# The boundary between gate-up groups: the order of pair 6's banks, of the additions and of pair 7's products

## The chip, the cores and the metric

The kernel runs on one core of a Trainium2 chip. The metric is the device time of one execution in microseconds (us). In the profile PE is TensorE's matmul, PEld its weight load, DVE is VectorE, ACT is ScalarE, POOL is GpSimd and SP is SyncE, whose queue issues most of the loads. A source line of the kernel before is named by L and its number; DMA is a transfer.

## The reference

One layer of a hybrid encoder over 256 tokens of width 2048, in float32: a feed-forward layer, a mixer (a gated linear recurrence beside windowed attention), and a second feed-forward layer of the same form.

```python
def swiglu(x, w_gate_up, w_down):
    gate, up = jnp.split(x @ w_gate_up, 2, axis=-1)
    return (jax.nn.silu(gate) * up) @ w_down
...
    ff = swiglu(rms_norm(x, pre_norm_ffn1[layer]), w_ffn1_gate_up[layer], w_ffn1_down[layer])
    x = x + 0.5 * rms_norm(ff, post_norm_ffn1[layer])
    ...
    ff = swiglu(rms_norm(x, pre_norm_ffn2[layer]), w_ffn2_gate_up[layer], w_ffn2_down[layer])
    x = x + 0.5 * rms_norm(ff, post_norm_ffn2[layer])
```

`w_gate_up` is 2048 x 11264, `w_down` 5632 x 2048. The change touches `x @ w_gate_up` alone, in both feed-forward layers.

## The kernel before

**Split products.** Each float32 operand is split into an upper part h (a cast to a shorter format, on ACT, L176) and a lower part l = raw - h (a subtraction, on DVE or POOL, L177). A full product is three matmuls: upper by upper, upper by lower, lower by upper (`three`, `some_of`, L447).

**Groups and pairs.** The gate-up matrix is worked in 11 groups of 512 gate and 512 up columns. A group sums over K = 2048 in 8 pairs of 256 rows. Its result is four banks of PSUM, 128 x 512 each: c[m][n], m the half of the tokens, n = 0 for gate and 1 for up. The names "pa" and "pb" in the profile are the two tags under which the banks are allocated; c[0][n] and p1, p5 are pa, c[1][n] and p6, p7 are pb.

**Plain pairs and pairs of seven.** A plain pair adds eight block products (24 matmuls) to the c banks. A pair of seven forms Strassen-like sums of blocks first and needs seven block products (21 matmuls): three go to c banks, four to side banks p1, p5, p6, p7, which are added to the c banks at the end of the group. Pairs 2 to 6 are of that kind in groups 3 to 10; in group 2 pairs 2, 4, 5 and 6; in group 1 some pairs, but not pair 6. Such a pair costs DVE two additions on the raw tile (L1001, L1002) and three or four subtractions; its weights come by two loads of SP and one adding load of POOL (`add_second`, L148), which `prepare` issues behind a split of the pair's first block (h1, l1).

**Order.** The engines' order is written by hand: every engine executes its instructions in the order in which the code records them (`manual_schedule`). The pools of h and l hold 5 tiles of 128 x 1024 each.

**The boundary.** `boundary` ends a group. `take` has issued pair 6's products, with `before_fold` in an order of their own. The eight additions of the side banks (through two rooms, a and b, named z and s in the profile) run on DVE, after a copy of p1 by ACT (L1259); between them stand pair 7's products, whose weights POOL has split (`splits(g, last, nc.gpsimd)`): `bank(m, n)` is the four matmuls of one bank that need no lower part of the weights (`upper`), and `lower()` the eight that do. Behind it `some(ahead, 2)` splits the next group's pair 0, and `first_pairs` goes on with the silu of the finished banks (`units`: L1176 on ACT, L1181 on DVE), the next group's pairs 0 and 1 and the transposes.

Of the kernel before, what the change touches and what calls it, by code (L numbers as in the profile page):

```python
# [17 lines left out]
ALU = mybir.AluOpType  # L18
# [30 lines left out]
def hymba_layer_kernel(  # L49
# [19 lines left out]
    nc = tc.nc  # L69
# [145 lines left out]
    last = {}  # L215
# [186 lines left out]
    class Blocks:  # L402
# [4 lines left out]
        ahead = None  # L407
# [27 lines left out]
        def bank(self, at):  # L435
            return self.p[at[1]] if at[0] == "p" else self.c[at[1]][at[2]]
# [486 lines left out]
    class Gated(Blocks):  # L923
# [91 lines left out]
        def take_parted(self, g, u):  # L1015

            (h0, l0), (h1, l1) = self.split_of.pop((g, u))
            del self.raws[g, u]
            a = self.tiles[u]

            def parts(m, n, k):
                ms = slice(m * P, (m + 1) * P)
                o = (n ^ k) * 512
                cs = slice(o, o + 512)
                return ("c", m, n), a[:, k, 0, ms], a[:, k, 1, ms], (h0, h1)[k][:, cs], (l0, l1)[k][:, cs]

            def upper(m, n):
                for k in range(2):
                    at, ah, al, h, _ = parts(m, n, k)
                    self.some_of(at, (ah, h), (al, h))  # L1030

            def lower():
                for k in range(2):
                    for n in range(2):
                        for m in range(2):
                            at, ah, _, _, l = parts(m, n, k)
                            self.some_of(at, (ah, l))

            return upper, lower

        def take(self, g, u):

            got = self.split_of.pop((g, u))
            del self.raws[g, u]
            first = self.firsts.pop((g, u), None)
            if first:
                before_fold = u == KT // 2 - 2
                self.products(u, first, *got, (0, 1, 3, 4, 5, 6, 2) if before_fold else range(7))
                return ()
            hs, ls = zip(*got)  # L1050
            return [
                (lambda k=k, m=m, n=n: self.plain(u, hs, ls, m, n, k))
                for k in range(2)
                for m in range(2)
                for n in range(2)
            ]
# [27 lines left out]
    def ffn(gated, w_dn, post_gain, again, gain=None, lead=None, opening=None):  # L1084

        with ExitStack() as st:
# [136 lines left out]
            def some(steps, n):  # L1223
                for _ in range(n):
                    next(steps)

            last = KT // 2 - 1
# [24 lines left out]
            def boundary(g, ahead):  # L1252

                a, b = room_for("z"), room_for("s")
                c, (p1, p5, p6, p7) = gated.c, gated.p
                add = nc.vector.tensor_tensor
                bank, lower = gated.take_parted(g, last)

                nc.scalar.copy(a, p1)  # L1259
                add(c[0][0], c[0][0], a, ALU.add)  # L1260
                add(b, p6, a, ALU.add)  # L1261
                add(a, p7, b, ALU.add)  # L1262
                add(c[1][0], c[1][0], a, ALU.add)  # L1263
                bank(0, 0)
                bank(1, 0)
                add(b, p5, b, ALU.subtract)
                add(c[0][1], c[0][1], b, ALU.add)  # L1267
                bank(0, 1)
                add(b, p5, a, ALU.subtract)  # L1269
                add(c[1][1], c[1][1], b, ALU.add)  # L1270
                bank(1, 1)
                lower()
                some(ahead, 2)

            def first_pairs(g, waiting, ahead):

                gated.group(g)
                sevens = FIVE if g in FIVE_IN else MIXED_IN
                if ahead:
                    some(waiting, 2)  # L1280
                    gated.prepare(g, sevens[1], nc.gpsimd)
                    some(ahead, 1)
                else:
                    some(waiting, 1)
                    gated.prepare(g, sevens[1])
                    some(waiting, 1)
                    ahead = gated.splits(g, 1)
                    some(ahead, 2)
                    gated.prepare(g, sevens[2])
                for one in gated.take(g, 0):  # L1290
                    one()
                some(waiting, 1)
                ahead = gated.splits(g, 2)
                some(ahead, 2)
                next(ahead, None)
                some(waiting, 1)
                for one in gated.take(g, 1):
                    one()
# [39 lines left out]
            raws, firsts, got = {}, {}, {}  # L1338
# [73 lines left out]
            with tc.manual_schedule():  # L1412
                if not opening:
                    gated.prepare(1, MIXED_IN[0])
                    some(gated.splits(1, 0), 2)
                begun = None
                for g in range(1, NG):
                    first_pairs(g, waiting, begun)
                    for u in range(2, last - 1):
                        pair_ahead(g, u)  # L1420
                    some(gated.splits(g, last, nc.gpsimd), 2)
                    for one in gated.take(g, last - 1):
                        one()
                    boundary(g, gated.splits(g + 1, 0) if g < NG - 1 else splits(0))
                    if g < NG - 1:
                        begun = gated.splits(g + 1, 1)
                        next(begun)
                    among = None
                    if g < NG - 1:
                        third = (FIVE if g + 1 in FIVE_IN else MIXED_IN)[2]  # L1430
                        among = lambda g=g, u=third: gated.prepare(g + 1, u, nc.gpsimd)
                    waiting = units(gated.c, rest, among)
                    some(waiting, 2)
                room_cm.__exit__(None, None, None)
                close_far()
                back_cm = tc.tile_pool(name=nm("hb"), bufs=AWAY // 2, reuse_waits="tile")
                back = back_cm.__enter__()
                fetch_at = {2: (1,), 4: (3,), 6: (0,), 8: (5,), 10: (2,), 12: (7,), 13: (4,), 15: (6,)}
                fetch_at.update({25: (3,), 26: (0,), 28: (5,), 29: (1,)})
                again_at = {4: 16, 7: 17, 10: 18, 30: 19}  # L1440
                for u in (*MIXED[8:], 17):
                    sums[u] = None
                rows = Pairs(w_dn, orders, hts, sums, work, post_gain, near=MIXED[:2])
                rows.firsts = 3
                some(waiting, 2)
                ahead = splits(1)
                some(ahead, 2)
                products(0)
                for _ in range(2):
                    load_down(back.tile([P, 2048], F32, tag="raw", name=nm("raw"), bufs=2))  # L1450
                some(waiting, 1)
                ahead = splits(2)
                some(ahead, 2)
                some(waiting, 1)
                some(ahead, 1)
                products(1)
                for i in range(2, 2 * NU - Pairs.HELD):
                    if i == NU + 18:
                        back_cm.__exit__(None, None, None)
                        early_cm.__exit__(None, None, None)  # L1460
                        post = rows.post = st.enter_context(post_pool())
                    ahead = splits(i + 1)
                    next(ahead, None)
                    prepare(i + 4)
                    for u in fetch_at.get(i, ()):
                        fetch(u)
                    next(ahead, None)
                    if i == NU + 18:
                        rows.hold(1, raws[2 * NU - 2])
                    products(i)  # L1470
                    for _ in ahead:
                        pass
                    if i in again_at:
                        sums[again_at[i]] = sums_again(again_at[i])
                    if i == 8:
                        rows.half_gain(far["pool"])
                    if i == NU - 1:
                        sums[19] = None
                        rows.second_run()
                        rows.fold_after(NU - Pairs.HELD - 1)  # L1480
                fold = rows.fold()
                some(fold, 2)
                rows.hold(1, raws[2 * NU - 1])
                for _ in fold:
                    pass
# [8 lines left out]
    gated = Gated(w_ffn1_gate_up, two_banks())  # L1494
    xt = new_xt()
    gated.see(xt)
    with tc.manual_schedule():
# [17 lines left out]
        first = gated.source(0)  # L1515
# [1043 lines left out]
```

## Time and profile before

| | us |
|---|---|
| median of 3 runs (1822.75 to 1824.27) | 1823.04 |
| the profiled execution | 1823.13 |
| its span in the profile | 1821.4 |
| PE busy | 1798.4 (99%) |
| DVE busy | 1648.0 (90%) |
| ACT busy | 1143.9 (63%) |
| POOL busy | 288.5 (16%) |

How to read it: the span is the time from the first to the last instruction of the profiled execution, and 1.7 us lie around it. The granted clock is 0.999 of full speed. PE is busy nearly all of the span, so a microsecond counts where PE idles or where its matmuls start further apart than they must. A group of the gate-up stage takes about 42.4 us (pair 6 of one group starts at 381.23, pair 6 of the next at 423.63), and there are 10 boundaries in each of the two layers. The fused rows of the timeline start at the first of their instructions and last to the end of the last.

### The profile page before, as it was taken

What the parts mean: (1) busy time and instruction counts of PE and PEld (TensorE: products, weight loads), DVE (VectorE), ACT (ScalarE), POOL (GpSimd) and SP (SyncE); (2) the same over time, 40 slices, a digit from 0 to 9 for tenths busy, and PEclk for the clock granted to TensorE, in tenths of its full rate; (3) what the DMA queues carried; (4) which work ended last, traced back from release to release, by engine and by line L of the source; (5) the groups of instructions that cost most, each with busy time, mean ns of one, the idle gap of its engine ahead of it and who ended that gap; (6) DMA issues with size and microseconds to landing.
All of it is one profiled execution on the core that took longest, in us unless ns stands there. A gap on an engine that the chain in (4) does not pass through costs nothing.

```text
span 1821.4 us, 24095 instructions
## 1 busy us (share of the span) xinstructions
PE 1798.4 (99%) x8320; PEld 1480.1 (81%) x8320; DVE 1648.0 (90%) x2154; ACT 1143.9 (63%) x1527; POOL 288.5 (16%) x270
## 2 busy tenths in 40 slices
PE   9999999999999999999999999999999999999998
PEld 7877787777788888888899888877777778788886
DVE  6899999999999999888888888889999999999997
ACT  7556666666665667566667566556666656566663
POOL 0122322222110100000000000022223222200110
PEclk9999999999999999999999999999999999999999
DMA  9789999899799997954555767889999899799895
GB/s 369 231 246 283 284 296 261 262 256 253 237 325 306 310 281 244 295 160 165 181 166 173 254 206 262 249 236 270 285 278 279 255 270 260 199 319 340 270 318 167
DMA packets 130331, 469.05 MB, mean 258 GB/s; under 512 B 14608, under 2 KB 17424, under 8 KB 128672
## 3 DMA queue, kind: packets, MB, share of 16 engines
q1 hardware_dynamic: 109152, 391.18, 59.5%
q0 software_dynamic: 20912, 76.07, 23.5%
q8 instruction: 65, 1.06, 0.2%
q14 instruction: 58, 0.48, 0.1%
q10 hardware_dynamic: 144, 0.26, 0.0%
HBM read 452.77 MB, written 14.68 MB: 257 GB/s over the span
## 4 chain that ended last, share of the span: by engine, by line
PE 86%; DVE 9%; DMA 2%; ACT 1%; issue 1%; SPq 0%; POOL 0%; DVEq 0%; ACTq 0%; POOLq 0%
PE pa L447 39%; PE pb L447 34%; PE pa L315 6%; PE pa L320 3%; DVE l L177 1%; DMA raw<-in_w_ffn_gate_up_dram 1%; ACT h L176 1%; DVE pa L1267 1%; DVE pb L1270 1%; DVE s L1269 1%; DVE z L1262 1%; DVE pb L1263 1%; PE pa L369 1%; DVE s L1261 1%; PE pa L368 1%
## 5 line engine op out<-in xcount | busy, mean ns | idle before, releaser
L176 ACT CAST h<-raw 128x1024 fp32r<-128x1024 f32 (+1 forms) x881 | 850.6, 1002 | 428.2 <-DVE raw L1002 99.8
L177 DVE TENSOR_TENSOR l<-raw,h 128x1024 fp32r<-128x1024 f32 (+1 forms) x789 | 915.6, 1191 | 64.3 <-ACT h L176 45.5
L447 PE MATMUL pa<-h,xt 128*128 128x512 f32 x1214 | 407.9, 393 | 4.3 <-DVE pa L1267 3.9
L447 PE MATMUL pb<-h,xt 128*128 128x512 f32 x1012 | 350.9, 395 | 7.2 <-DVE pb L1270 5.4
L447 PEld LDWEIGHTS pa<-h,xt 128*128 128x128 f32 x1214 | 226.3, 188 | 59.0 <-DVE pa L1267 12.8
L447 PEld LDWEIGHTS pb<-h,xt 128*128 128x128 f32 x1012 | 186.8, 188 | 61.1 <-DVE pb L1270 14.1
L447 PE MATMUL pa<-l,xt 128*128 128x512 f32 x583 | 227.6, 390 | 0.4 <-DVE l L177 0.4
L447 PE MATMUL pb<-l,xt 128*128 128x512 f32 x506 | 197.1, 389 | 0.0
L177 POOL TENSOR_TENSOR l<-raw,h 128x1024 fp32r<-128x1024 f32 (+1 forms) x76 | 142.7, 1897 | 207.7 <-ACT h L176 202.4
L447 PE MATMUL pb<-h,ht 128*128 128x512 f32 x428 | 151.2, 389 | 0.0
L447 PE MATMUL pa<-h,ht 128*128 128x512 f32 x428 | 151.1, 389 | 0.0
L148 POOL DMA_DIRECT2D raw<-in_w_ffn_gate_up_dram x93 | 81.7, 890 | 420.1 <-DVE l L177 369.5
L447 PEld LDWEIGHTS pa<-l,xt 128*128 128x128 f32 x583 | 109.5, 188 | 23.4 <-DVE l L177 1.4
L447 PE MATMUL pa<-h,xs 128*128 128x512 f32 x328 | 117.5, 389 | 0.5 <-DVE sums L399 0.5
L447 PE MATMUL pb<-h,xs 128*128 128x512 f32 x328 | 114.3, 389 | 0.0
L447 PEld LDWEIGHTS pb<-l,xt 128*128 128x128 f32 x506 | 95.0, 188 | 19.8
L315 PE MATMUL pa<-xt,h 128*128 128x512 f32 x448 | 109.9, 393 | 0.0
L315 PEld LDWEIGHTS pa<-xt,h 128*128 128x128 f32 x448 | 81.5, 188 | 15.3
L447 PEld LDWEIGHTS pb<-h,ht 128*128 128x128 f32 x428 | 80.3, 188 | 16.6
L447 PEld LDWEIGHTS pa<-h,ht 128*128 128x128 f32 x428 | 80.3, 188 | 16.6
L148 POOL DMA_DIRECT2D raw<-in_w_ffn_down_dram x42 | 36.5, 868 | 348.0 <-DVE la L177 276.8
L447 PE MATMUL pa<-l,ht 128*128 128x512 f32 x214 | 83.3, 389 | 0.0
(345 smaller groups left out, 2681.5 us busy)
## 6 DMA issues: line engine op xcount, KB each, us to landing
raw<-in_w_ffn_gate_up_dram SPq DMA_DIRECT2D x350, 512.0 KB, 6.4
raw<-in_w_ffn_down_dram SPq DMA_DIRECT2D x176, 512.0 KB, 8.5
raw<-in_w_mix_in_dram SPq DMA_DIRECT2D x94, 512.0 KB, 4.8
raw<-in_w_ffn_gate_up_dram POOLq DMA_DIRECT2D x93, 512.0 KB, 8.9
raw<-in_w_ffn_down_dram POOLq DMA_DIRECT2D x42, 512.0 KB, 8.7
ht<-away SPq DMA_DIRECT2D x24, 512.0 KB, 10.5
raw<-in_w_mix_out_dram SPq DMA_DIRECT2D x24, 512.0 KB, 5.9
away<-ht SPq DMA_DIRECT2D x16, 512.0 KB, 9.2
```

The costliest lines, as they stand in the source:

```text
L148: nc.gpsimd.dma_start(raw[:, 0:1024], src[:, 512:1536], accum_op=ALU.add)
L176: nc.scalar.copy(hi, src)
L177: by.tensor_tensor(lo, src, hi.bitcast(F32), ALU.subtract)
L315: nc.tensor.matmul(slot[f], weights(hs, kk, f), xcol(xt, k), start=(k == 0), stop=(k == KT - 1))
L320: nc.tensor.matmul(slot[f][:, 0:T], weights(ls, kk, f), xcol(xt, kh * 8 + kk, 0), start=False, stop=False,)
L368: nc.tensor.matmul(dst, xh, l[:, o : o + n], start=False, stop=False)
L369: nc.tensor.matmul(dst, xl, h[:, o : o + n], start=False, stop=(k == KT - 1))
L447: nc.tensor.matmul(self.bank(at), lhs, rhs, start=(n == 1), stop=n in (ends, self.of[at]), skip_group_check=n > ends,)
L1261: add(b, p6, a, ALU.add)
L1262: add(a, p7, b, ALU.add)
L1263: add(c[1][0], c[1][0], a, ALU.add)
L1267: add(c[0][1], c[0][1], b, ALU.add)
```

## The change

Pair 6 (`take`): its side-bank products come first (p1, p5, p7, p6) and the three products for c banks behind them; before, one c product stood in second place. Boundary: ACT copies p1 before it casts pair 7's weights, not after; the eight additions stand in one row with b = p6 + a first; and each of pair 7's banks takes its product with the first half of the lower parts right behind its four upper ones (`most`). The products with the second half follow: of three banks ahead of the last bank's products, of the last bank at the end. `first_pairs`: the second split of pair 1 (`some(ahead, 1)`) is recorded ahead of `prepare`, not behind it. No instruction is added or removed.

```diff
-            def lower():
-                for k in range(2):
-                    for n in range(2):
-                        for m in range(2):
-                            at, ah, _, _, l = parts(m, n, k)
-                            self.some_of(at, (ah, l))
+            def lower(m, n, k):
+                at, ah, _, _, l = parts(m, n, k)
+                self.some_of(at, (ah, l))
...
-                self.products(u, first, *got, (0, 1, 3, 4, 5, 6, 2) if before_fold else range(7))
+                self.products(u, first, *got, (0, 3, 4, 5, 1, 6, 2) if before_fold else range(7))
...
-                bank, lower = gated.take_parted(g, last)
-
                 nc.scalar.copy(a, p1)
+                some(gated.splits(g, last, nc.gpsimd), 2)
+                upper, lower = gated.take_parted(g, last)
+
+                def most(m, n):
+                    upper(m, n)
+                    lower(m, n, 0)
+
+                add(b, p6, a, ALU.add)
                 add(c[0][0], c[0][0], a, ALU.add)
-                add(b, p6, a, ALU.add)
                 add(a, p7, b, ALU.add)
                 add(c[1][0], c[1][0], a, ALU.add)
-                bank(0, 0)
-                bank(1, 0)
+                most(0, 0)
+                most(1, 0)
                 add(b, p5, b, ALU.subtract)
                 add(c[0][1], c[0][1], b, ALU.add)
-                bank(0, 1)
+                most(0, 1)
                 add(b, p5, a, ALU.subtract)
                 add(c[1][1], c[1][1], b, ALU.add)
-                bank(1, 1)
-                lower()
+                for m, n in ((0, 0), (1, 0), (0, 1)):
+                    lower(m, n, 1)
+                most(1, 1)
+                lower(1, 1, 1)
                 some(ahead, 2)
...
                 if ahead:
                     some(waiting, 2)
+                    some(ahead, 1)
                     gated.prepare(g, sevens[1], nc.gpsimd)
-                    some(ahead, 1)
...
-                    some(gated.splits(g, last, nc.gpsimd), 2)
                     for one in gated.take(g, last - 1):
                         one()
```

PE, pair 7 of group 8 in the first layer, before. The c banks are pa_3090, pb_3092, pa_3091, pb_3093; h_3363, h_3367 and l_3364, l_3368 are the upper and lower parts of pair 7's two halves.

```order
L447 MATMUL pa_3090<-h_3363,xt_125 128x512 x2
L447 MATMUL pa_3090<-h_3367,xt_125 128x512 x2
L447 MATMUL pb_3092<-h_3363,xt_125 128x512 x2
L447 MATMUL pb_3092<-h_3367,xt_125 128x512 x2
L447 MATMUL pa_3091<-h_3363,xt_125 128x512 x2
L447 MATMUL pa_3091<-h_3367,xt_125 128x512 x2
L447 MATMUL pb_3093<-h_3363,xt_125 128x512 x2
L447 MATMUL pb_3093<-h_3367,xt_125 128x512 x2
L447 MATMUL pa_3090<-l_3364,xt_125 128x512
L447 MATMUL pb_3092<-l_3364,xt_125 128x512
```

The same place on PE now, from the second bank on (the parts are h_3387, h_3391, l_3388, l_3392; ahead of these rows stand the same five for pa_3090).

```order
L447 MATMUL pb_3092<-l_3388,xt_125 128x512
L447 MATMUL pa_3091<-h_3387,xt_125 128x512 x2
L447 MATMUL pa_3091<-h_3391,xt_125 128x512 x2
L447 MATMUL pa_3091<-l_3388,xt_125 128x512
L447 MATMUL pa_3090<-l_3392,xt_125 128x512
L447 MATMUL pb_3092<-l_3392,xt_125 128x512
L447 MATMUL pa_3091<-l_3392,xt_125 128x512
L447 MATMUL pb_3093<-h_3387,xt_125 128x512 x2
L447 MATMUL pb_3093<-h_3391,xt_125 128x512 x2
L447 MATMUL pb_3093<-l_3388,xt_125 128x512
```

Each bank has five products instead of four before the next bank's begin, and the last bank has three more ahead of it; the first lower part is needed at the fifth product instead of the seventeenth.

ACT at the same boundary, before: the cast for pair 6's last part (h_3356), the two of pair 7, the copy of p1, then the next group's pair 0 and the silu.

```order
L176 CAST h_3356<-raw_489 128x1024
L176 CAST h_3363<-raw_495 128x1024
L176 CAST h_3367<-raw_495 128x1024
L1259 COPY z_3394<-pa_3210 128x512
L176 CAST h_3429<-raw_486 128x1024
L176 CAST h_3433<-raw_486 128x1024
L176 CAST h_3439<-raw_489 128x1024
L1176 ACTIVATE z_3443<-pa_3090,scales 128x512
L1176 ACTIVATE s_3445<-pb_3092,scales 128x512
L176 CAST h_631_3453<-raw_483 128x512
L176 CAST h_3458<-raw_489 128x1024
```

ACT there now.

```order
L176 CAST h_3356<-raw_489 128x1024
L1254 COPY z_3384<-pa_3210 128x512
L176 CAST h_3387<-raw_495 128x1024
L176 CAST h_3391<-raw_495 128x1024
L176 CAST h_3429<-raw_486 128x1024
L176 CAST h_3433<-raw_486 128x1024
L176 CAST h_3439<-raw_489 128x1024
L1173 ACTIVATE z_3443<-pa_3090,scales 128x512
L1173 ACTIVATE s_3445<-pb_3092,scales 128x512
L176 CAST h_3453<-raw_489 128x1024
L176 CAST h_633_3459<-raw_483 128x512
```

The copy of p1 moved ahead of pair 7's two casts, and the short cast of `prepare` (128x512) moved behind a long one of pair 1.

## The prediction

> **What bounds the kernel now.** I read the page first, then the waits, then the timeline of one boundary engine by engine (group 8 of the first layer, which I call by its start, S = 381.23), and last the same rows of other boundaries.
>
> ```profile
> PE 1798.4 (99%) x8320; PEld 1480.1 (81%) x8320; DVE 1648.0 (90%) x2154; ACT 1143.9 (63%) x1527; POOL 288.5 (16%) x270
> ```
>
> PE is the bound, and DVE stands close behind it. What PE waits for:
>
> ```profile
> PE pb L447 <- DVE pb L1270: 5.4, 20, 0.3
> PE pa L447 <- DVE pa L1267: 3.9, 18, 0.5
> PE pb L447 <- DVE pb L1263: 0.9, 3, 0.4
> ```
>
> Nearly all of it is the additions of `boundary`, at 18 places: 9 in each layer. The one missing is group 1, whose side banks are complete a pair earlier. Those 10.2 us understate the loss, as a busy row lasts until its matmul drains. The starts tell it better. PE at S (pair 6 first, pair 7 from 385.99, the next group from 392.82):
>
> ```profile
> 381.23 0.39 PE L447 MATMUL pa<-h,xt 128*128 128x512 f32 x1
> ...
> 384.18 0.39 PE L447 MATMUL pb<-l,xs 128*128 128x512 f32 x1
> 384.40 0.39 PE L447 MATMUL pb<-h,xs 128*128 128x512 f32 x1
> ...
> 385.99 1.07 PE L447 MATMUL pa<-h,xt 128*128 128x512 f32 x4
> 387.11 1.19 PE L447 MATMUL pb<-h,xt 128*128 128x512 f32 x4
> 388.50 1.20 PE L447 MATMUL pa<-h,xt 128*128 128x512 f32 x4 [0.20 <-DVE pa L1267]
> 389.96 1.20 PE L447 MATMUL pb<-h,xt 128*128 128x512 f32 x4 [0.26 <-DVE pb L1270]
> ...
> 392.82 0.39 PE L447 MATMUL pa<-h,xt 128*128 128x512 f32 x1
> ```
>
> Pair 6's 21 products take 4.76 us, 0.227 each, without a gap. At that pace pair 7's 24 would take 5.44; they take 6.83, so 1.39 are lost. The banks start 1.12, 1.39 and 1.46 apart where four products need 0.91: each waits for its additions. DVE there:
>
> ```profile
> 380.07 2.95 DVE L177 TENSOR_TENSOR l<-raw,h 128x1024 fp32r<-128x1024 f32 x3
> 383.73 0.70 DVE L1260 TENSOR_TENSOR pa<-pa,z 128x512 f32<-128x512 f32 x1 [0.70 <-ACT z L1259]
> 384.83 0.69 DVE L1261 TENSOR_TENSOR s<-pb,z 128x512 f32<-128x512 f32 x1 [0.40 <-PE pb L447]
> 386.35 0.70 DVE L1263 TENSOR_TENSOR pb<-pb,z 128x512 f32<-128x512 f32 x1
> 389.81 3.48 DVE L177 TENSOR_TENSOR l<-raw,h 128x1024 fp32r<-128x1024 f32 x3
> 395.10 2.60 DVE L177 TENSOR_TENSOR l<-raw,h 128x1024 fp32r<-128x1024 f32 x2 [0.48 <-ACT h L176]
> 406.16 0.69 DVE L1001 TENSOR_TENSOR raw<-raw 128x512 f32<-128x512 f32 x1 [1.63 <-DMA raw<-in_w_ffn_gate_up_dram]
> ```
>
> b = p6 + a (L1261) starts 0.04 after p6's last product (384.40 + 0.39) has ended; from it to the end of the row seven additions take 4.98, 0.71 each. PE resumes 0.06 after an addition ends (L1263 at 387.05, PE at 387.11). A bank needs two additions, 1.42, and gives PE 0.91 of work: that is the loss.
>
> The first and the last of the 18 (the first two rows, the second two) show the same distances:
>
> ```profile
> 131.17 1.07 PE L447 MATMUL pa<-h,xt 128*128 128x512 f32 x4
> 135.13 1.20 PE L447 MATMUL pb<-h,xt 128*128 128x512 f32 x4 [0.27 <-DVE pb L1270]
> ...
> 1581.46 1.07 PE L447 MATMUL pa<-h,xt 128*128 128x512 f32 x4
> 1585.43 1.20 PE L447 MATMUL pb<-h,xt 128*128 128x512 f32 x4 [0.27 <-DVE pb L1270]
> ```
>
> I take 1.40 for each, 18 x 1.40 = 25.2 us: all that this change could bring.
>
> **The change, part by part.** *Pair 6's order.* p6 is complete with the 12th product instead of the 15th, 0.68 earlier: b starts at S+2.92 instead of S+3.60. c[0][0]'s own product is now the fifth and ends at about S+3.56, when DVE is ready for its addition.
>
> *Additions in one row.* Eight of 0.71 from S+2.92 end at S+8.6, as before (389.90 is S+8.67): c[0][0] complete at 4.3, c[1][0] at 5.8, c[0][1] at 7.2, c[1][1] at 8.6. *Pair 7 on PE:* c[0][0] at S+4.76, no wait; five products, 1.13: c[1][0] at 5.89, with its additions done at 5.8 + 0.06, no wait; c[0][1] would come at 7.03 but may start at 7.2 + 0.06, a wait of 0.2 and, as behind each wait now, 0.1 until the pace is back; then eight products, so c[1][1] at 9.1, its additions long done. Loss 0.3 instead of 1.4: 18 x 1.1 = 19.8 us.
>
> *Casts and first lower part.* ACT and POOL now:
>
> ```profile
> 380.27 2.95 ACT L176 CAST h<-raw 128x1024 fp32r<-128x1024 f32 x3 [1.06 <-DVE raw L1002]
> 383.12 0.57 ACT L1259 COPY z<-pa 128x512 f32<-128x512 f32 x1
> 392.34 0.69 ACT L1176 ACTIVATE z<-pa,scales 128x512 f32<-128x512 f32 x1 [4.83 <-PE pa L447]
> 393.49 3.47 ACT L176 CAST h<-raw 128x512 fp32r<-128x512 f32 x4
> ...
> 383.23 4.79 POOL L177 TENSOR_TENSOR l<-raw,h 128x1024 fp32r<-128x1024 f32 x2
> 394.19 1.30 POOL L177 TENSOR_TENSOR l<-raw,h 128x512 fp32r<-128x512 f32 x1 [6.17 <-ACT h L176]
> ```
>
> The first row holds three casts, 0.98 each: pair 6's last and pair 7's two. The copy can start when p1 is complete (third product, about S+0.9) and ends at S+1.5; pair 7's casts end at S+2.5 and S+3.4, before S+4.76. POOL's two subtractions (2.4 each) then end near S+5.0 and S+7.4; they are needed at the fifth product, S+5.67, and the sixteenth, S+8.5. This costs nothing while the 0.7 of cover lasts; behind it stands PE itself. Moved with the casts are the two loads of SP that refill pair 7's raw tile: SP has nothing between the old place and the new, but they start when POOL has read the tile, some 0.6 later than 388.02. That tile is cast again behind the next group's transposes, over 10 us on, so I cost it at nothing; without that cover it would be 0.6 on ACT.
>
> *Silu and `prepare`.* The silu needs c[0][0] and c[1][0] complete, now at about S+8.9 instead of 392.34 (S+11.1). ACT then does the long cast, then `prepare`'s short one: the long one is ready at S+11.1, so DVE's 0.48 of waiting at 395.10 goes. POOL's short subtraction starts about 1.2 earlier than 394.19, and its adding load with it, so L1001 at 406.16 can come earlier by as much. The swap in `first_pairs` takes 1.0 of the silu's 2.2 back; the refill of pair 1's raw tile, which SP issues with that split, comes before POOL's adding load instead of after it, on another queue, and I cost that at nothing too.
>
> *What is late next.* DVE ends its boundary at the same S+8.6, while PE starts the next group 1.1 earlier. Behind 406.16 DVE works without a pause until pair 6, whose last lower part PE needs at the 14th product; now it is the 11th. How close that was, DVE's row (three subtractions, its end counts) and the PE product that reads it; at S 384.18 - 383.02 = 1.16. The first of 18, the tightest, the last:
>
> ```profile
> 124.82 2.95 DVE L177 TENSOR_TENSOR l<-raw,h 128x1024 fp32r<-128x1024 f32 x3
> 129.35 0.39 PE L447 MATMUL pb<-l,xs 128*128 128x512 f32 x1
> ...
> 1491.28 2.96 DVE L177 TENSOR_TENSOR l<-raw,h 128x1024 fp32r<-128x1024 f32 x3
> 1494.56 0.39 PE L447 MATMUL pb<-l,xs 128*128 128x512 f32 x1
> ...
> 1575.58 2.50 DVE L177 TENSOR_TENSOR l<-raw,h 128x1024 fp32r<-128x1024 f32 x2
> 1579.65 0.39 PE L447 MATMUL pb<-l,xs 128*128 128x512 f32 x1
> ```
>
> Margins 1.58, 0.32 and 1.57; over the 18 they average 1.05. Each loses 0.68 (three products) and 1.1 (the shorter period) and regains 0.48: -1.30. With 0.04 for the handover the new stall is 1.34 minus the old margin: 0.2 at a middling boundary, 1.0 at the tightest, none at the widest. Averaged, with none below zero and the places that waited for the earlier landing eased, I take 0.28: 18 x 0.28 = 5.0 us.
>
> **The sum.** 25.2 - 5.4 - 5.0 = 14.8 us saved. The profiled execution took 1823.13 (span 1821.4 and 1.7 around it), 0.1 above the median 1823.04: 1823.1 - 14.8 = 1808.3, say 1808.
>
> **The rivals.** *PE's gain comes whole* (DVE's slack covers the next group; for it speaks the idle 1.63 at 406.16, against it the margin of 0.32 at the tightest boundary): 19.8 saved, 1803.3.
>
> *DVE gives nothing back* (its 0.48 reappears as another wait, or the load lands no earlier): each margin falls by 1.78, the average stall is 1.78 + 0.04 - 1.05 = 0.77, 13.9 in all, and 25.2 - 5.4 - 13.9 = 5.9 are left: 1817.2. For it speaks DVE's 90%.
>
> *The loads set the pace,* and nothing changes. Two rows bear on it, waits of ACT and one whole group:
>
> ```profile
> ACT h L176 <- DMA raw<-in_w_ffn_gate_up_dram: 55.2, 38, 4.8
> 381.23:423.63 42.40, 41.89 (x186) 33.83 (x185) 38.33 (x45) 25.55 (x32) 11.96 (x10) 1.00 0.90 258
> ```
>
> The DMA engines are busy 0.90 of the 42.40 us; a period of 41.3 makes it 0.92. ACT does wait for landings, but no wait of PE for ACT stands in the view. If the landings hold the period, 1823.
>
> *POOL blocks DVE,* and it is slower. POOL's short subtraction (1.30) now falls among DVE's subtractions at about S+11.7, where before it ran beside L1181 and the idle 0.48. The row at 395.10 shows the little overlap there is: two subtractions in 2.60 while POOL ends its own at 395.49, against 3.48 for three at 389.81, 0.28 more than two at that pace. If DVE had to sit out the whole 1.30 at each boundary, in a group where DVE is the bound, 18 x 1.30 = 23.4 would be lost: 1808.3 + 23.4 = 1831.7. It decides from 14.8 / 18 = 0.82 a boundary. Against it: DVE's three subtractions follow each other without a gap, so POOL more likely waits than blocks, and the silu's products that come next read PSUM.
>
> The Trainium skill, "SBUF — State Buffer", section "Who interferes with whom", says that a DVE instruction with two SBUF inputs and a GpSimd instruction that reads SBUF hold the shared port pair exclusively, and that the one issued first blocks the other for its whole length. By that rule with POOL first, the time is this rival's 1831.7; with DVE first it is POOL that waits, and the forecast stands. The row at 395.10 agrees in kind: the 0.28 is less than the 0.39 for which POOL still ran.
>
> **How the numbers follow.** Forecast 0.58 (its own range 1805 to 1812: the 0.28 a boundary may be 0.1 or 0.5); whole gain 0.16; DVE gives nothing back 0.14; loads 0.06; POOL blocks 0.06. The first three are faster by over 0.2% (3.6 us, about what a measurement of this kernel tells from no change): 0.88; same 0.06; slower 0.06. The range reaches over the first three cases: 1802 to 1817.5.
>
> **What would show it.** Right: PE's wait for the last addition (L1270's successor) gone, one wait of about 0.2 for c[0][1]; pair 7 in 5.7 us; new waits of PE for DVE's l in pair 6 of the later groups, up to 1 us; the group's period at about 41.5. Wrong: POOL's first subtraction named as what PE waits for at the fifth product; the idle before L1001 grown; DVE's subtractions behind the silu lengthened to 2 us and more.

## The result and the profile after

The changed kernel takes 1804.28 us (median of 4 runs, 1804.23 to 1806.16) against 1822.89 for the kernel before in the same comparison: 18.6 us less, a ratio of 0.990 (95% interval 0.9882 to 0.9917). The forecast was 1808.3, so the gain was foreseen in kind and came 3.8 us larger. The profiled execution took 1804.27, with a span of 1802.5; against the profiled one of before the span is 18.9 shorter. Source lines of the changed kernel differ a little: the additions of `boundary` are L1262 to L1272 there, the silu L1173 and L1178, the copy of p1 L1254.

The page's line on the engines, after:

```profile
PE 1790.9 (99%) x8320; PEld 1481.4 (82%) x8320; DVE 1641.9 (91%) x2154; ACT 1145.8 (64%) x1527; POOL 291.3 (16%) x270
```

PE's busy sum fell by 7.5 us though it executes the same 8320 matmuls. A matmul that must wait for an addition is partly counted as busy, so neither the busy sum nor the waits are the gain; the starts are. The waits of PE, in us in all, times, longest:

```profile
PE pb L116 <- DVE idle L110: 1.4, 1, 1.4
...
PE pa L447 <- DVE pa L1269: 0.3, 1, 0.3
...
PE pb L447 <- DVE pb L1265: 0.2, 1, 0.2
```

The 20 waits for the last addition (5.4 us) are gone, and of the 18 for the one before (3.9) one of 0.3 is left; the first row stands at the kernel's start and was there before. The timeline of PE at the same boundary (group 8, now S = 374.66; pair 7 from 379.51, the next group from 385.32):

```profile
379.51 1.07 PE L447 MATMUL pa<-h,xt 128*128 128x512 f32 x4
380.42 0.39 PE L447 MATMUL pa<-l,xt 128*128 128x512 f32 x1
380.64 1.17 PE L447 MATMUL pb<-h,xt 128*128 128x512 f32 x4
381.65 0.39 PE L447 MATMUL pb<-l,xt 128*128 128x512 f32 x1
382.02 1.19 PE L447 MATMUL pa<-h,xt 128*128 128x512 f32 x4
...
383.96 1.07 PE L447 MATMUL pb<-h,xt 128*128 128x512 f32 x4
...
385.32 0.39 PE L447 MATMUL pa<-h,xt 128*128 128x512 f32 x1
```

Pair 7 takes 5.81 where it took 6.83; 5.44 would be without loss. DVE, then POOL, then ACT around it:

```profile
377.71 0.69 DVE L1262 TENSOR_TENSOR s<-pb,z 128x512 f32<-128x512 f32 x1 [0.90 <-PE pb L447]
...
383.33 3.48 DVE L177 TENSOR_TENSOR l<-raw,h 128x1024 fp32r<-128x1024 f32 x3
386.73 0.75 DVE L1178 SCALAR_TENSOR_TENSOR z<-pa,scales,z 128x512 f32<-128x512 f32 x1
388.05 2.35 DVE L177 TENSOR_TENSOR l<-raw,h 128x1024 fp32r<-128x1024 f32 x2
398.95 0.69 DVE L1001 TENSOR_TENSOR raw<-raw 128x512 f32<-128x512 f32 x1 [1.72 <-DMA raw<-in_w_ffn_gate_up_dram]
...
386.61 1.37 POOL L177 TENSOR_TENSOR l<-raw,h 128x512 fp32r<-128x512 f32 x1 [4.66 <-ACT h L176]
...
383.71 0.69 ACT L1173 ACTIVATE z<-pa,scales 128x512 f32<-128x512 f32 x1 [2.67 <-PE pa L447]
```

The silu comes at S+9.05 (before S+11.11). DVE's two subtractions behind it follow its products without the wait of 0.48 and take 2.35 instead of 2.60. POOL's short subtraction falls at S+11.95, just as DVE's three subtractions end, and runs beside the silu's products (two of L1178, to 388.05). The whole group, in us, with the busy time of PE, PEld, DVE, ACT and POOL, then the granted clock, the DMA engines' busy share and GB/s:

```profile
374.66:416.14 41.48, 41.48 (x187) 33.82 (x186) 38.01 (x45) 25.81 (x32) 12.09 (x10) 1.00 0.92 261
```

The typical period is 41.40, down from 42.40, with the DMA engines at 0.92.

**Two boundaries that the prediction left out.** The row of the waits before read "5.4, 20", and there are 20 boundaries, not 18. PE at the end of group 1, before (first two rows: first product of pair 7, first of the next group) and after:

```profile
88.11 1.07 PE L447 MATMUL pa<-h,xt 128*128 128x512 f32 x4
...
94.91 0.39 PE L447 MATMUL pa<-h,xt 128*128 128x512 f32 x1
```

```profile
87.95 1.07 PE L447 MATMUL pa<-h,xt 128*128 128x512 f32 x4
...
93.39 0.39 PE L447 MATMUL pa<-h,xt 128*128 128x512 f32 x1
```

6.80 before, 5.44 after: the group loses nothing any more. Both layers have it, 2 x 1.4.

**The account.** The loss at a boundary is the time from the first product of pair 6 to the first of the next group, less 45 products at 0.227. Before, 18 boundaries lost 26.3 in all (three of them 1.7) and group 1's two 2.8: 29.1. After, pair 7 loses 7.6 at the 18 (0.39 each, two of them 0.74) and pair 6's new waits for DVE's lower parts take 3.1; group 1 loses nothing. 29.1 - 10.7 = 18.4 of the span's 18.9.

Pair 6's 3.1 lie at eight of the 18 boundaries, up to 0.81 at one. No row of the waits shows them, since the product ahead of a short wait still counts as busy. At the boundary that loses most, the fifth and the eleventh product of pair 6 come late (first product of pair 6, the fourth, the two late ones, the first of pair 7):

```profile
1475.16 0.39 PE L447 MATMUL pa<-h,xt 128*128 128x512 f32 x1
...
1475.84 0.39 PE L447 MATMUL pa<-h,xs 128*128 128x512 f32 x1
1476.32 0.50 PE L447 MATMUL pa<-l,xs 128*128 128x512 f32 x1
...
1478.06 0.50 PE L447 MATMUL pb<-l,xs 128*128 128x512 f32 x1
...
1480.73 1.07 PE L447 MATMUL pa<-h,xt 128*128 128x512 f32 x4
```

Pair 6 takes 5.57 there where 4.76 is its pace.

### The profile page after: what moved, and what is told of

Same layout as the page of the kernel before. It is cut to its first block, busy times and chain, and to the rows that moved or that the text cites. A ratio compares the mean times of both kernels' runs of the same rounds, so it can differ in the third digit from the quotient of the medians.

```text
span 1802.5 us, 24099 instructions
## 1 busy us (share of the span) xinstructions
PE 1790.9 (99%) x8320; PEld 1481.4 (82%) x8320; DVE 1641.9 (91%) x2154; ACT 1145.8 (64%) x1527; POOL 291.3 (16%) x270
## 4 chain that ended last, share of the span: by engine, by line
PE 74%; DVE 10%; issue 6%; DMA 5%; ACT 2%; POOL 2%; SPq 0%; DVEq 0%; ACTq 0%; POOLq 0%
PE pa L447 33%; PE pb L447 28%; PE pa L315 6%; DVE l L177 5%; DMA raw<-in_w_ffn_gate_up_dram 3%; PE pa L320 3%; ACT h L176 2%; DVE raw L1001 2%; DMA away<-ht 1%; POOL l L177 1%; DVE raw L1002 1%; PE pa L369 1%; PE pa L368 1%; PE pa L367 1%; PE pb L1858 1%
```

## The experiments

Each changes the kernel after in a few places; ratios are to the kernel before in the same comparison (its medians lie between 1822.89 and 1823.52), and "the changed kernel" is at 1804.28.

**1. Pair 6's old order.**

```diff
-(0, 3, 4, 5, 1, 6, 2) if before_fold
+(0, 1, 3, 4, 5, 6, 2) if before_fold
```

> The changed kernel with pair 6's old order (one c product in second place), all else as changed. Theory A (start of the additions and filler of PE work between them add up): p6 is complete 0.68 us later, so each bank is ready 0.68 later while PE arrives as early as now; pair 7 loses about 1.05 instead of 0.40 at the 18 boundaries whose pair 6 is one of seven: +11.7 us; the 3.1 us that PE now waits for DVE in pair 6 go, since its last part is needed three products later: about 1813. Rival B (the five products per bank carry the gain by themselves): 1804 to 1806. Rival C (the order of pair 6 carries it): near 1820.

1813.63 (1813.48 to 1814.46), ratio 0.9949 (0.9936 to 0.9962): theory A's time. PE's waits:

```profile
PE pa L447 <- DVE pa L1263: 3.4, 18, 0.2
```

The additions start three products later, so PE waits for c[0][0] as well, at 18 boundaries. By the starts each loses 1.07 instead of 0.39, and the waits in pair 6 are gone: 18 x 0.68 - 3.1 = 9.1 of the 9.35 measured. Undone alone, the early start of the additions is worth half of the gain.

**2. Pair 7's old order of products.**

```diff
-                most(0, 0)
-                most(1, 0)
+                upper(0, 0)
+                upper(1, 0)
...
-                for m, n in ((0, 0), (1, 0), (0, 1)):
-                    lower(m, n, 1)
-                most(1, 1)
-                lower(1, 1, 1)
+                upper(1, 1)
+                for k in range(2):
+                    for n in range(2):
+                        for m in range(2):
+                            lower(m, n, k)
```

> The changed kernel with pair 7's old order: four products per bank, the eight with lower parts at the end; all else as changed. Theory A: additions done at S+4.3, 5.8, 7.2, 8.6 (S: start of pair 6), PE has 0.91 of work a bank, waits of about 0.3, 0.5 and 0.6: loss about 1.25 instead of 0.40 at 20 boundaries, +17, less the 3.1 of waits in pair 6: about 1818. Rival B (five products carry it): 1820 or more. Rival C (the order of pair 6 and the early additions carry it): 1804 to 1808.

1825.54 (1824.11 to 1826.5), ratio 1.0012 (1.0003 to 1.0021): on the rival's side, and slower even than the kernel before. Each of the 18 boundaries loses 1.40 again. The additions do start early, but their row ends at S+8.68 where nothing delayed it, as in the kernel before (S+8.67), and PE still has 12 products to do behind the last of them. Pair 6 still waits for DVE, 5.2 us in all. One boundary's rows, DVE's and POOL's, and DVE's subtractions of the whole run (busy us, mean ns):

```profile
311.99 1.99 DVE L177 TENSOR_TENSOR l<-raw,h 128x1024 fp32r<-128x1024 f32 x1 [0.25 <-ACT h L176]
...
311.08 1.82 POOL L177 TENSOR_TENSOR l<-raw,h 128x512 fp32r<-128x512 f32 x1 [6.82 <-ACT h L176]
...
L177 DVE TENSOR_TENSOR l<-raw,h 128x1024 fp32r<-128x1024 f32 (+1 forms) x789 | 927.1, 1205 | 59.6 <-ACT h L176 41.1 <-issue 6.9 <-PE pa L320 4.9
```

A single subtraction of DVE takes 1.99 where 1.16 to 1.23 is usual (a third of the 3.48 for three is 1.16), and POOL's short one 1.82 where 1.30 is usual: they lie on each other, and do so at all 16 boundaries at which POOL has that subtraction (the two at the end of a layer have none). Neither theory had that. Experiment 9 takes it up.

**3. Without the exchange in `first_pairs`.**

```diff
-                    some(ahead, 1)
                     gated.prepare(g, sevens[1], nc.gpsimd)
+                    some(ahead, 1)
```

> The changed kernel with the old order in first_pairs: prepare's short cast ahead of pair 1's second long one. Theory A: POOL's adding load goes out about 1.0 earlier, DVE's first subtraction behind the silu (388.05 in the trace) has its cast by 386.6: no new wait; the idle before L1001 shrinks where there is one, 1803.3 to 1804.5. Rival D (POOL's short subtraction, now about 385.6 to 386.9 among DVE's three, blocks DVE): up to 1.3 a boundary, 1810 or more.

1817.38 (1813.1 to 1822.77), ratio 0.9967 (0.9955 to 0.998): the rival on POOL and DVE. The profiled execution has a span of 1811.6, 9.1 above the changed kernel's. DVE, POOL, PE's waits, and PE in the pair 6 that follows:

```profile
346.28 4.60 DVE L177 TENSOR_TENSOR l<-raw,h 128x1024 fp32r<-128x1024 f32 x3
...
348.51 1.29 POOL L177 TENSOR_TENSOR l<-raw,h 128x512 fp32r<-128x512 f32 x1 [4.11 <-ACT h L176]
...
PE pa L447 <- DVE l L177: 5.3, 7, 1.2
...
381.35 0.50 PE L447 MATMUL pa<-l,xs 128*128 128x512 f32 x1 [1.20 <-DVE l L177]
```

POOL's subtraction comes 1.0 earlier and lands among DVE's three, which take 4.60 instead of 3.48. DVE does not make up for that 1.1 before the next pair 6, and PE waits there, 30 us later. Not all of the 1.20 comes from the meeting: on its way DVE also waits 0.86 for a load at L1001 (368.71), 0.20 at the same place in the changed kernel.

That is the course at nine of the 16 boundaries. At the other seven it is POOL that pays. DVE and POOL one group later:

```profile
389.53 3.49 DVE L177 TENSOR_TENSOR l<-raw,h 128x1024 fp32r<-128x1024 f32 x3
...
391.78 2.40 POOL L177 TENSOR_TENSOR l<-raw,h 128x512 fp32r<-128x512 f32 x1 [3.75 <-ACT h L176]
```

DVE keeps its time, and POOL takes 1.1 more than its 1.29. The recorded starts differ by very little: POOL's lies 0.03 to 0.04 ahead of DVE's third subtraction at the nine, 0.02 ahead at the seven. Nine times 1.12 is 10.1 us of DVE's time. The losses of the 18 boundaries add up to 19.75 instead of 10.7, which is the 9.1 of the spans. The seven executions spread from 1813.10 to 1822.77, and the profiled one (1813.38) is among the fastest; more boundaries at which DVE pays would make such a difference, but no other execution was traced, so this is not shown.

**4. Pair 7's casts ahead of pair 6, as before the change.**

```diff
-                some(gated.splits(g, last, nc.gpsimd), 2)
...
+                    some(gated.splits(g, last, nc.gpsimd), 2)
                     for one in gated.take(g, last - 1):
```

> The changed kernel with pair 7's two casts ahead of pair 6's products and of the copy of p1, as before the change. Theory A: the copy ends at S+2.5 to 3.1 instead of S+1.5, and is needed at S+2.9 to 3.6, so it costs 0 to 0.3 a boundary: 1804.3 to 1808. Rival E (the copy's place is a main part of the gain): the additions start 0.7 later everywhere, 1815 or more.

1804.86 (1803.92 to 1805.58), ratio 0.9898 (0.9884 to 0.9912): not told apart from the changed kernel. The copy then ends later, but at all 18 boundaries the first addition still starts 0.11 behind the end of p6's last product, with the copy done by then; one boundary of group 1 loses 0.3.

**5. The next group's first short subtraction by POOL.**

```diff
-                    gated.prepare(g + 1, MIXED_IN[0])
+                    gated.prepare(g + 1, MIXED_IN[0], nc.gpsimd)
```

> The changed kernel with the subtraction of the next group's first prepared block (128x512, 0.68 us on DVE ahead of pair 6's last part) done by POOL instead. Theory A (PE's waits in pair 6 come from DVE's backlog): DVE ends pair 6's last part 0.68 earlier, the 3.1 us of waits go: 1801. Rival D (POOL and DVE subtractions block each other): the 1.3 of POOL falls among DVE's subtractions of pair 6; no gain or a loss, 1804 to 1815.

1810.65 (1809.38 to 1812.03), ratio 0.993 (0.9917 to 0.9942), in the rival's range. DVE was to be relieved of 0.68 and lost instead; DVE's two additions on the raw tile and POOL's subtraction:

```profile
375.15 0.69 DVE L1001 TENSOR_TENSOR raw<-raw 128x512 f32<-128x512 f32 x1
375.88 1.67 DVE L1002 TENSOR_TENSOR raw<-raw 128x512 f32<-128x512 f32 x1
...
375.23 1.77 POOL L177 TENSOR_TENSOR l<-raw,h 128x512 fp32r<-128x512 f32 x1 [10.04 <-ACT h L176]
```

L1002 ends 0.98 late, more than the 0.68 that was moved away. Pair 6's waits grow from 3.1 to 8.7.

**6. That subtraction behind pair 6's last part, on DVE.** The split of the next group's first block is recorded behind the last lower part of pair 6, and its adding load between POOL's two subtractions for pair 7.

```diff
-        def prepare(self, g, u, by=nc.vector):
+        def prepare(self, g, u, by=nc.vector, adds=True):
...
-            add_second(raw, self.source(u, g))
+            if adds:
+                add_second(raw, self.source(u, g))
...
-                some(gated.splits(g, last, nc.gpsimd), 2)
+                lasts = gated.splits(g, last, nc.gpsimd)
+                next(lasts)
+                if g < NG - 1 and MIXED_IN[0] in gated.here[g + 1]:
+                    u = MIXED_IN[0]
+                    add_second(gated.raws[g + 1, u], gated.source(u, g + 1))
+                next(lasts)
...
-                    gated.prepare(g + 1, MIXED_IN[0])
...
+                if u == last - 2 and g < NG - 1:
+                    gated.prepare(g + 1, MIXED_IN[0], adds=False)
```

> The changed kernel with that block's split recorded behind pair 6's last part, still on ACT and DVE, and its adding load between POOL's two subtractions for pair 7. Theory A: pair 6's last part 0.68 earlier, b not later (DVE idles 0.9 there): the 3.1 us of waits in pair 6 go, 1801; the load goes out about 4 us later and lands near S+15, just before L1001 at S+16. Rival F (it lands too late, or POOL's second subtraction, 0.9 later, becomes what PE waits for): 1805 to 1812.

1802.22 (1801.18 to 1802.51), ratio 0.9883 (0.9869 to 0.9896). Pair 6's waits fall from 3.1 to 0.4, and the median by 2.1: theory A in kind, a little short of its 1801.

**7. The last bank's upper products at the head of pair 7.** c[1][1] takes its products ahead of its additions, so they cover DVE's row.

```diff
+                upper(1, 1)
...
-                most(1, 1)
+                lower(1, 1, 0)
```

> The changed kernel with the last bank's four upper products at the head of pair 7, ahead of its additions (products and additions may come in either order), its two lower ones at the end. Theory A: PE has 0.91 more work before each of the other banks, the waits for c[1][0] and c[0][1] (0.40 a boundary) go: 8.0 less; but DVE keeps its end, so PE's waits in pair 6 grow by up to 0.4 at about half of the boundaries, 4 us: 1800. Rival G (DVE's backlog takes all of it): 1804.

1803.83 (1802.81 to 1805.62), ratio 0.9895 (0.9879 to 0.991): no gain on the changed kernel. One boundary on PE: first product of pair 6, the one that waits, first of pair 7, first of the next group.

```profile
1475.52 0.39 PE L447 MATMUL pa<-h,xt 128*128 128x512 f32 x1
...
1476.98 0.50 PE L447 MATMUL pa<-l,xs 128*128 128x512 f32 x1 [0.40 <-DVE l L177]
...
1481.35 1.07 PE L447 MATMUL pb<-h,xt 128*128 128x512 f32 x4
...
1486.79 0.39 PE L447 MATMUL pa<-h,xt 128*128 128x512 f32 x1
```

Pair 7 takes 5.44, no loss at all, at every boundary; pair 6 takes 5.83 here instead of 4.76, and 9.0 us are lost in it over the run (3.1 after the change). Of the 7.6 us won in pair 7, 5.9 came back in pair 6 (9.0 - 3.1): most of it, though not all as the rival had it, and more than the 4 of theory A. The medians differ by 0.45, within the spread of the runs.

**8. 6 and 7 together.**

> The two edits together: the last bank's upper products first, and the next group's first block split behind pair 6's last part. Theory A: both terms, 8.0 and 3.1, without the growth of the waits in pair 6: 1793 to 1795. Rival G (DVE or the landings set the pace whatever PE does): 1799 or more.

1796.61 (1795.9 to 1797.47), ratio 0.9853 (0.984 to 0.9867): 7.7 below the changed kernel, the fastest of all, and between the two theories (1793 to 1795, and 1799 or more). PE at group 8, and two whole groups:

```profile
371.94 0.39 PE L447 MATMUL pa<-h,xt 128*128 128x512 f32 x1
...
376.80 1.07 PE L447 MATMUL pb<-h,xt 128*128 128x512 f32 x4
...
382.24 0.39 PE L447 MATMUL pa<-h,xt 128*128 128x512 f32 x1
```

```profile
371.94:413.05 41.11, 41.11 (x187) 33.97 (x185) 39.55 (x46) 27.07 (x33) 12.45 (x10) 1.00 0.94 272
413.05:454.06 41.01, 41.01 (x186) 34.05 (x185) 38.53 (x44) 26.08 (x31) 12.47 (x10) 1.00 0.89 248
```

Pair 6 takes 4.86, pair 7 5.44. 2.3 us are lost at the boundaries in all, all of it in pair 6. A group without loss takes 41.01, with PE busy throughout and DVE 0.94 of it: in such a group PE alone sets the pace.

**9. Experiments 2 and 3 together.**

> Both undone: pair 7's products in the old order (four upper ones a bank, all eight lower ones at the end) and prepare ahead of the second split of the next group's pair 1. Pair 6's order, the additions' order and the earlier copy of p1 stay. With the old products alone and the exchange kept the time was 1825.5, with 1.40 lost at each of 18 boundaries as in the kernel before and about 6 us of waits of pair 6 for DVE's subtractions on top; there POOL's short subtraction (1.82) fell into DVE's (1.99 instead of 1.22). Theory A: the excess over the kernel before is that meeting of POOL and DVE. Without the exchange the short subtraction runs beside the silu's products as before (1.30), DVE's two subtractions behind the silu take 2.6 and not 3.5 with their wait, pair 6's waits shrink to 1 to 3 us, and the time is 1821 to 1823.5. Then the exchange is worth about 12 with the new products and costs about 3 with the old: its worth hangs on when the silu comes. Rival B: the excess comes from pair 6's order alone (its last lower part is needed 0.68 earlier), whatever POOL does: pair 6's waits stay near 6 us and the time 1825 to 1826.

1822.6 (1821.2 to 1823.11), ratio 0.9995 (0.9986 to 1.0004): theory A's time, and not told apart from the kernel before. With the old products, then, pair 6's order, the row of additions and the earlier copy gain nothing that these runs can tell. DVE and POOL behind the silu, and DVE's subtractions of the whole run:

```profile
309.98 2.61 DVE L177 TENSOR_TENSOR l<-raw,h 128x1024 fp32r<-128x1024 f32 x2 [0.48 <-ACT h L176]
...
309.07 1.30 POOL L177 TENSOR_TENSOR l<-raw,h 128x512 fp32r<-128x512 f32 x1 [5.79 <-ACT h L176]
...
L177 DVE TENSOR_TENSOR l<-raw,h 128x1024 fp32r<-128x1024 f32 (+1 forms) x789 | 915.8, 1192 | 66.0 <-ACT h L176 47.6 <-issue 6.9 <-PE pa L320 4.8
```

Against experiment 2 the 789 subtractions take 11.3 less, pair 6's waits fall from 5.2 to 1.6, and 2.9 us are won. So the same exchange costs 2.9 with the old products and saves 13.1 with the new ones (9.1 by the profiled spans).

## Why the prediction was right, and where it was off

- *What bounds the kernel: right in kind, mis-sized.* The loss was additions against four products a bank. "I take 1.40 for each, 18 x 1.40 = 25.2" was too little by 3.9: the group 1 that it set aside lost 1.4 as well, in each layer, and three of the 18 lost 1.7. The cue was the 20 in the quoted row of the waits.
- *Pair 6's order: right.* The first addition starts at S+3.05 at group 8 (forecast S+2.92). Undone alone it costs 9.35.
- *Additions in one row, products interleaved: right, a little optimistic.* Pair 7 loses 0.39, not 0.3: c[1][0] waits 0.10 where none was forecast, c[0][1] 0.13 and 0.11 behind it. Over 18 boundaries 7.6 instead of 5.4, with 0.35 extra at two of them.
- *Casts at nothing: right.* No wait of PE for POOL stands in the view, and experiment 4 shows that the place of the casts is worth nothing.
- *What is late next: right place, smaller.* The new stall is where it was forecast, PE in pair 6 waiting for DVE's l, up to 0.81. It takes 3.1 and not 5.0. At group 8 the period fell by 0.9 to 1.0 (forecast 1.1), and L1001 came at S+24.29 instead of S+24.93, 0.64 earlier (forecast 0.48); the margin thus falls by some 1.05 instead of 1.30. Over the 18, the margin less the stall fell by 0.85 on average, 0.3 at the least and 1.6 at the most. A sign of being wrong, a longer idle before L1001, is there at group 8 (1.72, before 1.63) but not in the whole run: DVE's waits for loads at L1001 fell from 7.1 us (12 times) to 4.4 (7 times).
- *The sum.* 29.1 - 7.6 - 3.1 = 18.4 instead of 25.2 - 5.4 - 5.0 = 14.8: +3.9, -2.2 and +1.9. That the last two nearly cancel is luck.
- *The exchange in `first_pairs`: the valuation was wrong,* though it didn't reach the sum. "The swap takes 1.0 of the silu's 2.2 back" books it as a cost. Experiment 3 shows what it is for the time: without it POOL's short subtraction starts 2.23 behind the start of DVE's three (348.51 - 346.28), with it 3.28 behind (386.61 - 383.33), when they are all but done.
- *"POOL blocks DVE" at 0.06: it did not happen, but the mechanism is real,* and the argument against it ("POOL more likely waits than blocks") does not hold: in experiment 3 DVE pays 1.1 of POOL's 1.29 at nine boundaries of 16, and POOL waits at seven. What keeps the two apart in the changed kernel is the exchange. The rival's price was too high: 9 to 13, not 23.4. DVE was the one to pay at nine boundaries in the traced execution, not at 18, and paid 1.12 and not 1.30.
- *"PE's gain comes whole" and "DVE gives nothing back"* are neither what happened: pair 6's waits are 3.1, between the 0 of the one and the 13.9 of the other. The measured 1804.28 is nearer to the first one's 1803.3 than to the forecast only because the loss before was larger than counted. *"The loads set the pace"* is refuted: the period fell, and the DMA engines reach 0.94 in experiment 8 at 41.11 a group.

The parts do not add up. Undone one at a time, three of them cost 9.35, 21.3 and 13.1, together more than twice the 18.6 gained: each takes away what another rests on.

## What to carry to other kernels

When two engines are both above 90%, count a step's gain on the first and then the margin of the second, boundary by boundary; what is won without relieving the second is paid back at its next deadline (experiment 7), and kept only when that deadline is moved too (experiment 8). An instruction of POOL that reads SBUF is to be placed by time beside DVE work that reads PSUM, and a reordering that shifts it by a microsecond must be priced for that meeting, with either of the two paying (experiment 3). And count the places in the wait's own row before multiplying.

## What the runs showed of the hardware

POOL's short subtraction and a DVE instruction with two operands in SBUF did not run side by side, but for some 0.15 us. In experiment 5 POOL starts at 375.23 while L1001 of DVE ends at 375.84; POOL takes 1.77, 0.47 more than its 1.30, and L1002 behind ends 0.98 late. In experiment 3 DVE's three lose 1.12 while POOL keeps its 1.29 at nine boundaries; at seven DVE loses nothing and POOL takes 2.40. In experiment 2 both pay: 1.82 for 1.30 and 1.99 for 1.23. Beside the silu's products, which read a PSUM operand, POOL takes 1.30 (experiment 9) and DVE 0.74 to 0.75. In the changed kernel POOL takes 1.37 at group 8 and up to 1.49 elsewhere, where it starts up to 0.3 before DVE's third subtraction ends. The size was unexpected, and that within one execution now DVE pays and now POOL. The Trainium skill, "SBUF — State Buffer", section "Who interferes with whom", says that the two hold the shared port pair exclusively for a whole instruction, the first one blocking the other; these rows agree to about 0.15 us, with POOL first at nine boundaries of experiment 3 and DVE at seven, and each once in 2 and 5.

A wait of PE costs some 0.11 beyond itself: in the changed kernel the product that waited lasts 0.50 where 0.39 is usual (1476.32), and the next one starts 0.34 behind it (1476.66) where 0.227 is the pace.

Not settled: at two boundaries of a run (groups at 332.52 and 1391.99 after, 338.49 and 1406.42 before) an addition of DVE starts 0.46 late behind the one before it on its own engine, which costs PE 0.35. It stands at the same two groups in eight of the eleven kernels here, and not in experiments 5, 7 and 8. (The third boundary that lost 1.7 before, at 1491.62, has another cause: its row of additions starts late.) DVE in experiment 3:

```profile
344.21 0.70 DVE L1269 TENSOR_TENSOR pa<-pa,s 128x512 f32<-128x512 f32 x1 [0.46 <-DVE s L1268]
```

No run here tells what holds it.
